# A decoder layer on one core: the last norm's weights in the places of finished activations, and program order on three engines in the down projection's column passes

## The chip, the cores and the metric

The kernel runs on one NeuronCore of a Trainium2 chip. The metric is the device time of one execution in microseconds; the median of three runs before the change is 1082.98. A core has TensorE (PE, the matmuls), VectorE (DVE), ScalarE (ACT), GpSimd (POOL) and SyncE (SP, which here only issues DMAs). They run side by side and wait for each other through semaphores. Each takes its own instructions strictly in the order in which they were put into its queue, so a waiting instruction holds everything behind it on its engine.

## The reference, cut to what matters

```python
# x: (1, 256, 2048) float32; D_FF = 5632
x = x + rmsnorm(mix, post_mix_g)               # after the attention sub-layer
h = rmsnorm(x, pre_ffn_g)
u = causal_dwconv(h @ w_up, conv_w, conv_b)    # width 3 over the tokens
gate, val = jnp.split(u, 2, axis=-1)
y = (jax.nn.gelu(gate, approximate=True) * val) @ w_down    # (256, 5632) @ (5632, 2048)
x = x + rmsnorm(y, post_ffn_g)                 # post_ffn_g: the last norm's weights
```

## The kernel before, in words

Every float32 product is made of three products of split numbers: a weight tile is cast on ACT to a high part (`whi`), DVE subtracts that from the raw tile and gives a low part (`wlo`), and PE adds high x high, high x low and low x high (`product`, L992). So each loaded weight tile costs one DMA issued by SP, one cast on ACT (L333) and one subtraction on DVE (L334) before PE can use it.

The MLP is worked through in two halves of 22 row tiles of `w_down`. In each half, 11 groups of up projection, convolution, GELU and gate give 22 tiles `G` of activations (128 x 512, high and low part of 256 tokens), which take the 22 places of a tag of that name. Then comes the half's column stage: two passes (`column_pass`, L995 on), each over 1024 of the 2048 output columns. A pass goes over 11 pairs of G tiles in an order that is written out. Six pairs (`FAST`) use a scheme of seven products instead of eight block products (`seven`): the pair needs four weight forms, `b11` (512 wide), `f13`, `b2` and `f24` (1024 wide). `prepare` makes them: three loads, one of them of sums of weight rows that were formed in DRAM earlier; `f13` is split from it, then DVE adds to the same tile in place (L1019, L1020), and `f24` is split from the result, so the cast of `f24` waits for DVE and the subtraction for that cast. The other five pairs are plain: two loads, two splits, 24 matmuls. The last pair of a pass (the last three in the very last pass, `HOLD`) is held back and multiplied afterwards one output block at a time (`block`), so that each of the four output banks (`late`) is complete while PE goes on.

Four other banks (`m1`, `m5`, `m7`, `m6`) belong to the fast pairs alone. When the last fast pair, 7, is done, `add_early` adds them into the output `y_sb`: one copy on ACT, then four DVE operations in the first half, eight in the second. In the passes that hold one pair, the next pair's weights are prepared ahead of that; in the very last pass, `add_early` comes at the end of `run`, behind all the preparing. After a pass that is not the last, `ahead` prepares the next pass's first pair; then the four blocks follow, each with a DVE sum into `y_sb` (in the second half with a square on ACT, L1122).

Loads go in turn into five buffers `raw`, one `extra` and two `spare`; split weights go in turn into five pairs `whi`/`wlo` and further places that are free by then: in both halves the convolution's room (`slots`), in the second half also the place of `hT` (`more`), which held the up projection's input.

What sets the order: PE's instructions keep program order everywhere. For ACT, DVE, POOL and SP a scheduler chooses the order at build time, except where the code says otherwise; from the line `x_back = ...` on, all of them keep program order.

The tail: SP loads the residual (`x_back`, L1231) and then the last norm's weights, one tile of 128 x 2048 with the same row on all partitions (`gbf`, L1233), which takes the place of `hT`. POOL multiplies the output blocks by it (`gain`, L1203), takes the power for the norm (L1218), DVE adds the residual (`finish`, L1222), and SP and ACT issue the output DMAs. These steps are interleaved by hand with the last pass's four blocks; the last block is done in two halves of 256 columns.

Of the kernel before, what the change touches and what calls it, by code (L numbers as in the profile page):

```python
# [8 lines left out]
F32 = mybir.dt.float32  # L9
# [8 lines left out]
P = 128  # L18
# [14 lines left out]
def hybrid_layer(ctx: ExitStack, tc: tile.TileContext, x, pre_mix_g, w_in, b_forget, sinks,  # L33
# [834 lines left out]
    with tc.tile_pool(name="ffn", bufs=1) as fp:  # L868
# [47 lines left out]
        def conv(b, ch, dst_tag):  # L916
            u = ubuf[cnt[0] % NU]
# [7 lines left out]
                           scale=cw[:, 2, ch:ch + 1])  # L925
            dve.scalar_tensor_tensor(y, u[:, 1:257], cw[:, 1, ch:ch + 1], y, op0=ALU.mult,  # L926
# [68 lines left out]
        def column_pass(G, sums, weights, some, order, k00, c0, load, parts, hold=1):  # L995
# [14 lines left out]
            def prepare(u):  # L1010
# [33 lines left out]
            def run(add_early):  # L1044
                early, late = ([bank(tag) for _ in range(4)] for tag in ("acc", "att"))
                banks.extend(zip(late, (0, 0, 1, 1), (left, right, left, right)))
                for i, u in enumerate(order):
                    forms = ready.pop(u) if u in ready else prepare(u)
                    if u in some:
                        seven(u, forms, *early, *late[:3])  # L1050
                        if u == fast[-1] and hold == 1:
                            nxt = order[i + 1]
                            ready[nxt] = prepare(nxt)
                            add_early(*early)
# [8 lines left out]
                if hold > 1:  # L1063
                    add_early(*early)
# [8 lines left out]
            return ahead, run, block  # L1073

        ysq = [small.tile([P, 5], F32, tag=f"ysq{t}", bufs=1, name=f"ysq{t}") for t in range(2)]
        for half in range(2):
# [5 lines left out]
            for g in range(FHALF // 2):  # L1082
# [41 lines left out]
            slots = fp.tile([P, ROOM], F32R, tag="room", name="slots")  # L1124
            slots = [slots[:, 32 + i * UNIT:32 + (i + 1) * UNIT] for i in range(2)]
            if half:
                more = main.tile([P, 8, UNIT], F32R, tag="hT", name="more")
                slots += [more[:, i, :] for i in range(8)]
            extra = fp.tile([P, UNIT], F32, tag="extra", name="extra")
            spare = fp.tile([P, 2, UNIT], F32, tag="gates", name="spare")  # L1130
            turn = [None] * 5
            turns = turn + [extra] + turn
            turn = [spare[:, 0, :], spare[:, 1, :], extra] + turn
            units = [0]

            def load(src):
                if not turns:
                    turns.extend(turn)
                raw, c = turns.pop(0), src.shape[-1]
                if raw is None:  # L1140
                    return w_load(src, 1, c)[0]
                sp.dma_start(raw[:, :c].rearrange("p (a c) -> p a c", a=1), src)
                return raw

            def parts(src, n):
                i = units[0] % (5 + len(slots) // 2) - 5
                units[0] += 1
                hi, lo = w_parts(n) if i < 0 else [x[:, :n] for x in slots[i * 2:i * 2 + 2]]
                split(hi, lo, src[:, :n])
                return hi, lo  # L1150

            def y_of(t, n):
                return y_sb[:, t, n * 512:(n + 1) * 512]

            def early_sums(n):
                def add(m1, m5, m7, m6):
                    y11, y12, y21, y22 = (y_of(t, n + c) for t in range(2) for c in range(2))
                    if half == 0:
                        act.copy(y11, m1)
                        dve.tensor_tensor(y12, m6, y11, op=ALU.add)  # L1160
                        dve.tensor_tensor(y21, m7, y12, op=ALU.add)
                        dve.tensor_tensor(y12, m5, y12, op=ALU.subtract)
                        dve.tensor_tensor(y22, m5, y21, op=ALU.subtract)
                        return
                    s = fp.tile([P, 512], F32, tag="cst", name="s")
                    act.copy(s, m1)
                    dve.tensor_tensor(y11, s, y11, op=ALU.add)
                    dve.tensor_tensor(s, m6, s, op=ALU.add)
                    dve.tensor_tensor(y12, y12, s, op=ALU.subtract)
                    dve.tensor_tensor(y12, m5, y12, op=ALU.add)  # L1170
                    dve.tensor_tensor(s, m7, s, op=ALU.add)
                    dve.tensor_tensor(y21, s, y21, op=ALU.add)
                    dve.tensor_tensor(s, m5, s, op=ALU.subtract)
                    dve.tensor_tensor(y22, s, y22, op=ALU.add)
                return add

            weights = {u: pair_sums[half, u] for u in FAST}
            passes = [column_pass(G, sums, weights, FAST, order, half * FHALF, n * 512, load, parts,
                                  hold)
                      for n, order, hold in  # L1180
# [115 lines left out]
```

## Time and the profile before

| | us |
|---|---|
| median of 3 runs (1081.89 to 1084.2) | 1082.98 |
| profiled execution, its own time | 1084.41 |
| its span on the chip | 1082.7 |
| first half's column stage | 579.15 to 697.74 |
| second half's column stage | 940.02 to 1056.96 |
| PE's last matmul ends | 1056.96 |

The profile is one execution, taken by the hardware profiler. Times are from the span's start. Rows of a timeline give start, duration, engine, line and operation, output <- input, the count of instructions merged and, in brackets, the idle time before and what ended it. Busy time of pipelined instructions overlaps, so the step from one start to the next says more than a duration.

### The profile page before, as it was taken

The page shows a single profiled execution, that of the slowest core. Times are in us where ns is not written, and L with a number is a line of the kernel's source. Part 1 is how long each engine was busy: PE and PEld are TensorE (multiplying, and loading weights), DVE is VectorE, ACT ScalarE, POOL GpSimd, SP SyncE. Part 2 cuts the span into 40 slices and gives each one's busy share as a digit, 9 for nine tenths or more (in the row PEclk, how much of TensorE's full clock was granted, in tenths as well). Part 3 has the DMA queues.
Part 4 walks back from the last instruction along what each step waited for, and adds up shares of the span by engine and source line. Part 5 has one row for each costly group of instructions (what it writes and reads, how often), then busy time and mean ns, then how long its engine had stood idle before and what let it go on. Part 6 is the DMA issues. An engine that isn't in the chain of part 4 may idle for free.

```text
span 1082.7 us, 16421 instructions
## 1 busy us (share of the span) xinstructions
PE 1048.4 (97%) x5866; PEld 911.0 (84%) x5866; DVE 848.1 (78%) x1389; ACT 648.3 (60%) x1116; POOL 248.2 (23%) x280
## 2 busy tenths in 40 slices
PE   9999999999999999999999989999999999999990
PEld 7899988888889888888888878888888888878880
DVE  5988868886468788787878888768778887889963
ACT  7776757767467666565655645556555665656720
POOL 3254245440131222222221000013131222100004
PEclk9999999999999999999999989999999999999995
DMA  8748678765994987877876757769696866586733
GB/s 292 236 131 236 182 218 254 191 218 160 327 258 145 324 262 223 232 234 232 233 203 201 249 184 259 239 206 250 212 254 201 232 191 198 163 266 230 233 137 117
DMA packets 170798, 238.56 MB, mean 220 GB/s; under 512 B 7996, under 2 KB 132188, under 8 KB 169692
## 3 DMA queue, kind: packets, MB, share of 16 engines
q1 hardware_dynamic: 163184, 222.25, 63.7%
q0 software_dynamic: 6528, 12.58, 7.8%
q10 hardware_dynamic: 1004, 2.68, 0.6%
q8 instruction: 46, 0.75, 0.3%
q14 instruction: 36, 0.29, 0.1%
HBM read 233.14 MB, written 29.38 MB: 242 GB/s over the span
## 4 chain that ended last, share of the span: by engine, by line
PE 86%; DVE 7%; issue 3%; ACT 2%; DMA 1%; POOL 1%; SPq 0%; DVEq 0%; POOLq 0%; ACTq 0%
PE bank_acc L305 15%; PE bank_att L305 13%; PE bank_acc L330 12%; PE bank_att L992 10%; PE bank_acc L311 8%; PE bank_att L311 7%; PE bank_acc L274 7%; PE bank_acc L992 4%; PE bank_acc L279 4%; DVE wlo L334 2%; PE bank_att L496 1%; PE bank_att L531 1%; DVE wlo L136 1%; PE bank_acc L955 1%; DVE slots L334 1%
## 5 line engine op out<-in xcount | busy, mean ns | idle before, releaser
L136 DVE TENSOR_TENSOR wlo<-raw,whi 128x1024 fp32r<-128x1024 f32 (+3 forms) x271 | 331.4, 1235 | 110.1 <-ACT whi L133 103.4
L133 ACT CAST whi<-raw 128x1024 fp32r<-128x1024 f32 (+3 forms) x270 | 273.0, 1029 | 114.5 <-issue 65.5
L922 POOL TENSOR_TENSOR room<-room,rowf 128x256 f32<-128x256 f32 x88 | 99.2, 1147 | 368.5 <-DVE room L921 367.5
L305 PE MATMUL bank_acc<-hT,whi 128*128 128x512 f32 x736 | 173.3, 390 | 0.0
L305 PEld LDWEIGHTS bank_acc<-hT,whi 128*128 128x128 f32 x736 | 136.4, 188 | 27.4
L305 PE MATMUL bank_att<-hT,whi 128*128 128x512 f32 x640 | 150.6, 390 | 0.0
L305 PEld LDWEIGHTS bank_att<-hT,whi 128*128 128x128 f32 x640 | 118.7, 188 | 23.9
L992 PE MATMUL bank_att<-whi,G 128*128 128x512 f32 x298 | 99.4, 394 | 0.0
L924 ACT ACTIVATE room<-room,cw 128x256 f32<-128x256 f32 x88 | 52.9, 602 | 66.3 <-POOL room L922 66.3
L311 PEld LDWEIGHTS bank_acc<-hT,wlo 128*128 128x128 f32 x736 | 89.3, 188 | 2.0
L311 PE MATMUL bank_acc<-hT,wlo 128*128 128x256 f32 x736 | 89.9, 279 | 0.0
L274 PE MATMUL bank_acc<-hT,whi 128*128 128x512 f32 x352 | 88.0, 395 | 0.0
L330 PE MATMUL bank_acc<-whi,oT 128*128 128x512 f32 (+1 forms) x272 | 81.8, 379 | 0.0
L333 ACT CAST whi<-raw 128x1024 fp32r<-128x1024 f32 (+1 forms) x61 | 56.6, 957 | 39.3 <-PE bank_att L992 17.5
L334 DVE TENSOR_TENSOR wlo<-raw,whi 128x1024 fp32r<-128x1024 f32 (+1 forms) x61 | 66.5, 1117 | 16.1 <-ACT whi L333 16.1
L311 PEld LDWEIGHTS bank_att<-hT,wlo 128*128 128x128 f32 x640 | 77.6, 188 | 1.7
L311 PE MATMUL bank_att<-hT,wlo 128*128 128x256 f32 x640 | 77.9, 279 | 0.0
L926 DVE SCALAR_TENSOR_TENSOR room<-room,cw 128x256 f32<-128x256 f32 x88 | 61.4, 700 | 17.0 <-ACT room L924 16.9
L274 PEld LDWEIGHTS bank_acc<-hT,whi 128*128 128x128 f32 x352 | 63.3, 188 | 11.6
L992 PEld LDWEIGHTS bank_att<-whi,G 128*128 128x128 f32 x298 | 57.0, 191 | 12.1
L992 PE MATMUL bank_att<-wlo,G 128*128 128x512 f32 x149 | 58.7, 394 | 0.0
L330 PEld LDWEIGHTS bank_acc<-whi,oT 128*128 128x128 f32 x272 | 50.2, 188 | 9.4
(269 smaller groups left out, 1722.7 us busy)
## 6 DMA issues: line engine op xcount, KB each, us to landing
raw<-in_w_up_dram SPq DMA_DIRECT2D x176, 512.0 KB, 4.7
raw<-in_w_in_dram SPq DMA_DIRECT2D x51, 512.0 KB, 5.6
raw<-in_w_down_dram SPq DMA_DIRECT2D x45, 512.0 KB, 4.9
raw<-in_w_out_dram SPq DMA_DIRECT2D x32, 512.0 KB, 5.7
t<-in_w_down_dram SPq DMA_DIRECT2D x24, 512.0 KB, 7.3
t<-in_w_down_dram POOLq DMA_DIRECT2D x24, 512.0 KB, 8.7
spare<-in_w_down_dram SPq DMA_DIRECT2D x14, 512.0 KB
raw<-in_w_in_dram SPq DMA_DIRECT2D x16, 384.0 KB, 3.4
```

What stands on the lines that cost most here:

```text
L133: i1 = act.copy(hi[:, cs], raw[:, cs])
L136: i2 = dve.tensor_tensor(lo[:, cs], raw[:, cs], hi[:, cs].bitcast(F32), op=ALU.subtract)
L274: pe.matmul(b, parts[u][0][:, a, m * P:(m + 1) * P], hT[:, kt, :], start=(kt == 0), stop=(kt == KT - 1))
L305: pe.matmul(b, parts[u][0][:, a, m * P:(m + 1) * P], hT[:, kt, :], start=(kt == 0), stop=(kt == KT - 1))
L311: pe.matmul(b[:, 256:512], parts[u][1][:, a, m * P:(m + 1) * P], hT[:, kt, 0:256], start=False, stop=False)
L330: pe.matmul(b, a, r[:, cols], start=(first and i == 0), stop=(last and i == 2))
L333: act.copy(hi, src)
L334: dve.tensor_tensor(lo, src, hi.bitcast(F32), op=ALU.subtract)
L922: pool.tensor_tensor(u[:, 2:258], u[:, 2:258], rowf, op=ALU.mult)
L924: act.activation(y, u[:, 2:258], AF.Identity, bias=cw[:, 3, ch:ch + 1], scale=cw[:, 2, ch:ch + 1])
L926: dve.scalar_tensor_tensor(y, u[:, 1:257], cw[:, 1, ch:ch + 1], y, op0=ALU.mult, op1=ALU.add)
L992: pe.matmul(b[:, to] if to else b, a, r[:, cols], start=(first and i == 0), stop=(last and i == 2))
```

## The change

Three things are changed.

1. The last norm's weights are four tiles of 128 x 512 with the tag of `G`, so they take the places of G tiles 0 to 3 of the second half (pairs 0 and 1), and are loaded by four DMAs.
2. From the last group's convolution to the end of each half's column stage, ACT, DVE and SP keep program order. The code that makes the passes, their buffer turns and the early sums is moved up into functions; the turns themselves are the same. In the new order the first pass's pairs 1 and 3 are prepared ahead of the last group's convolution, which is cut into a beginning (copy, sum, POOL's product, activation) and an end, both beginnings first.
3. When pair 7 is done, in every pass the next two pairs of the order are prepared ahead of the early sums (before: the next one, and in the very last pass all). In the very last pass the early sums thereby come ahead of the preparing of pairs 9 and 10. In each pass's first fast pair, `f24` is split ahead of `b2`, as PE uses them in that order there.

```diff
+            return conv_end(*conv_begin(b, ch, dst_tag))
+        def conv_begin(b, ch, dst_tag):
...
             act.activation(y, u[:, 2:258], AF.Identity, bias=cw[:, 3, ch:ch + 1],
                            scale=cw[:, 2, ch:ch + 1])
+            return u, y, ch
+        def conv_end(u, y, ch):
...
-                b2, f24 = (parts(r, UNIT) for r in (r2, r13))
-                return b11, f13, b2, f24
-            def ahead():
-                ready[order[0]] = prepare(order[0])
+                if u == fast[0]:
+                    f24 = parts(r13, UNIT)
+                    return b11, f13, parts(r2, UNIT), f24
+                b2 = parts(r2, UNIT)
+                return b11, f13, b2, parts(r13, UNIT)
+            def ahead(*us):
+                for u in us:
+                    ready[u] = prepare(u)
...
-                        if u == fast[-1] and hold == 1:
-                            nxt = order[i + 1]
-                            ready[nxt] = prepare(nxt)
+                        if u == fast[-1]:
+                            ahead(*order[i + 1:i + 3])
                             add_early(*early)
...
-                if hold > 1:
-                    add_early(*early)
                 return late
...
+                if g == FHALF // 2 - 1:
+                    inner = tc.manual_schedule(engines={mybir.EngineType.Activation,
+                                                        mybir.EngineType.DVE,
+                                                        mybir.EngineType.SP})
+                    inner.__enter__()
+                    passes = column_passes()
+                    passes[0][0](1, 3)
+                    begun = [conv_begin(bv[m], 44 + c0 // P + m, "yv") for m in range(2)]
                 for m in range(2):
-                    y = conv(bv[m], 44 + c0 // P + m, "yv")
+                    if g == FHALF // 2 - 1:
+                        y = conv_end(*begun[m])
+                    else:
+                        y = conv(bv[m], 44 + c0 // P + m, "yv")
...
                 late = run(early_sums(n))
                 if n == 0:
-                    passes[1][0]()
-                elif half:
+                    passes[1][0](0)
+                elif not half:
+                    inner.__exit__(None, None, None)
+                else:
                     dve.tensor_tensor(y_of(1, 3), late[3], y_of(1, 3), op=ALU.add)
                     break
...
-                               gbf[:, n * 512:(n + 1) * 512][:, cs], op=ALU.mult)
+                               gbf[n][:, cs], op=ALU.mult)
...
+        inner.__exit__(None, None, None)
...
-        gbf = main.tile([P, D], F32, tag="hT", name="gbc_ffn")
-        sp.dma_start(gbf, post_ffn_g[0].partition_broadcast(P))
+        gbf = [fp.tile([P, 512], F32, tag="G", bufs=FHALF, name="gbc_ffn") for n in range(4)]
+        for n in range(4):
+            sp.dma_start(gbf[n], post_ffn_g[0][n * 512:(n + 1) * 512].partition_broadcast(P))
```

More of the change, by code (lines that the diff above doesn't have):

```diff
@@ new lines, in column_passes @@
+        def column_passes():
+            paused[0] = True
+            extra = fp.tile([P, UNIT], F32, tag="extra", name="extra")
+            raw_turns[:] = [None] * 5 + [extra] + [None] * 5
+            split_turns[:] = [None] * 5
+            cycles[:] = [extra], None
+            weights = {u: pair_sums[half, u] for u in FAST}
+            return [column_pass(G, sums, weights, FAST, order, half * FHALF, n * 512, load, parts,
+                                hold)
+                    for n, order, hold in
+                    ((0, (1, 3, 0, 2, 4, 8, 5, 6, 7, 9, 10), 1),
+                     (2, (0, 2, 4, 1, 5, 6, 7, 3, 8, 9, 10), HOLD) if half else
+                     (2, (0, 2, 1, 4, 5, 3, 6, 7, 8, 9, 10), 1))]
@@ L1122, in down @@
                 act.activation(junk[:, cs], ys, AF.Square, accum_out=ysq[t][:, i:i + 1])
[L1124 to L1180, printed above, removed]
-                      ((0, (1, 3, 0, 2, 4, 8, 5, 6, 7, 9, 10), 1),
-                       (2, (0, 2, 4, 1, 5, 6, 7, 3, 8, 9, 10), HOLD) if half else
-                       (2, (0, 2, 1, 4, 5, 3, 6, 7, 8, 9, 10), 1))]
-            paused[0] = True
+            more_places()
```

48 lines of the change are left out of this document (added).

## The prediction

> **What bounds the kernel now.** I read the page first, then the busy time by stretches of the two column stages and of the tail, then the timelines of those three places.
>
> ```profile
> span 1082.7 us, 16421 instructions
> PE 1048.4 (97%) x5866; PEld 911.0 (84%) x5866; DVE 848.1 (78%) x1389; ACT 648.3 (60%) x1116; POOL 248.2 (23%) x280
> 579.15:697.74 118.59, 115.66 (x494) 94.38 (x493) 100.89 (x117) 65.23 (x76) 1.99 (x6) 0.97 0.69 230
> 623.00:635.00 12.00, 9.29 (x28) 6.92 (x27) 9.90 (x13) 3.98 (x5) 0.00 (x0) 0.72 0.75 262
> 940.02:1056.96 116.94, 114.38 (x511) 94.24 (x509) 101.75 (x125) 65.63 (x84) 1.79 (x2) 0.99 0.61 207
> 953.00:961.00 8.00, 5.89 (x18) 4.43 (x18) 7.87 (x9) 4.37 (x6) 0.00 (x0) 0.79 0.80 260
> 1056.96:1082.70 25.74, 0.00 (x0) 0.00 (x0) 9.80 (x15) 1.74 (x6) 11.82 (x11) 0.55 0.34 123
> 680.74 17.00 PE bank_att L992 x75
> ```
>
> In the stretches the columns are length, busy time of PE, weight load, DVE, ACT, POOL, then granted clock, DMA share, GB/s. PE bounds the kernel until 1056.96; after it come 25.74 us in which PE does nothing. From the chain, 75 column matmuls take 17.00 us, 0.2267 each. A column stage has two passes; a pass has six seven-product pairs (21 matmuls) and five plain ones (24), 246 in all, so a stage at full clock without waits is 492 x 0.2267 = 111.5 us. The first half's stage takes 118.59: PE waits 118.59 - 115.66 = 2.9, and 4.2 go to the slow clock (0.72 at 623 to 635). The second takes 116.94: 2.6 of waiting, 2.8 of slow clock (0.79 at 953 to 961). DVE, at 101 to 102 us busy, is close behind PE in both stages. So the change can win in three places: two column stages and the tail.
>
> **The tail.**
>
> ```profile
> 1030.49 0.91 SPq L1231 DMA_DIRECT2D x_back<-x_dram  x2
> x_back<-x_dram SPq DMA_DIRECT2D x2, 1024.0 KB, 9.6
> 1056.99 0.33 SPq L1233 DMA_DIRECT2D gbc_ffn<-in_post_ffn_g_dram  x1
> gbc_ffn<-in_post_ffn_g_dram SPq DMA_DIRECT2D x1, 1024.0 KB, 4.7
> 1061.78 4.92 POOL L1203 TENSOR_TENSOR y_sb<-y_sb,gbc_ffn 128x512 f32<-128x512 f32 x4 [118.82 <-DMA gbc_ffn<-in_post_ffn_g_dram]
> 1073.83 0.41 DVE L1121 TENSOR_TENSOR y_sb<-bank_acc,y_sb 128x256 f32<-128x256 f32 x1
> ```
>
> The weights of the last norm lie in hT's place, which holds split weights that the last blocks read; their load leaves only at 1056.99, when PE is done. POOL then multiplies, and DVE, which in order waits for POOL, comes to the last half block's sum only at 1073.83. In G's places the load waits for pairs 0 and 1 of the last pass alone (its first and fourth), so it leaves right behind x_back. SP keeps its place: 1030.5, plus 9.6 for x_back, plus 4.7, gives weights by about 1045. Four issues instead of one add three of 0.33 on SP, with nothing behind them until the outputs. Before PE's end POOL then does six gains (4.92 / 4 = 1.23 each) and one power, under 8 us in some 12, each behind its block's sum. The last half block's sum starts 0.1 after PE's end instead of at 1073.83, that is 1073.83 - 1056.96 - 0.1 = 16.8 us earlier, and what follows (8.9 us to the end) stays. **Term: -16.8.** Its cover is POOL's 4 us of slack; without it the tail gives back what the gains are late, one for one.
>
> **Program order: what one pair costs DVE.**
>
> ```profile
> 954.44 1.21 DVE L334 TENSOR_TENSOR more<-extra,more 128x1024 fp32r<-128x1024 f32 x1
> 955.58 0.67 DVE L334 TENSOR_TENSOR wlo<-raw,whi 128x512 fp32r<-128x512 f32 x1
> 956.18 2.34 DVE L334 TENSOR_TENSOR wlo<-spare,whi 128x1024 fp32r<-128x1024 f32 x2
> 599.75 0.69 DVE L1019 TENSOR_TENSOR spare<-spare 128x512 f32<-128x512 f32 x1
> 600.47 0.69 DVE L1020 TENSOR_TENSOR spare<-spare 128x512 f32<-128x512 f32 x1
> 601.08 1.22 DVE L334 TENSOR_TENSOR slots<-raw,slots 128x1024 fp32r<-128x1024 f32 x1
> 662.94 2.36 DVE L334 TENSOR_TENSOR wlo<-raw,whi 128x1024 fp32r<-128x1024 f32 x2 [1.19 <-ACT whi L333]
> ```
>
> Start to start, a low part of 1024 takes 1.14, one of 512 0.60, the two sums 0.72 + 0.61. A seven-product pair is 0.60 + 3 x 1.14 + 1.33 = 5.35 on DVE (PE 21 x 0.2267 = 4.76), a plain one 2.28 (PE 5.44). Now DVE often idles 1.19 after the sums, waiting for the cast of what it has just summed (662.94). In program order the low part of r2 lies between, and the wait goes, except in each pass's first fast pair, where f24 now comes first: 1.2 there.
>
> ```profile
> 579.12 0.65 ACT L920 COPY room<-bank_acc 128x256 f32<-128x256 f32 x2 [0.49 <-PE bank_acc L305]
> 580.98 0.60 ACT L924 ACTIVATE room<-room,cw 128x256 f32<-128x256 f32 x1 [0.68 <-POOL room L922]
> 580.47 1.02 DVE L334 TENSOR_TENSOR wlo<-raw,whi 128x512 fp32r<-128x512 f32 x1
> 586.88 0.42 DVE L334 TENSOR_TENSOR G<-room,G 128x256 fp32r<-128x256 f32 x1
> ```
>
> The last group's convolution pays. ACT's second copy (0.3 behind the first now) must in order wait behind the first activation, 580.98 + 0.60; DVE's second sum follows it, and low parts no longer fill the gaps (the one at 580.47 did). I count the convolution done 7.5 us after the first column matmul (now 586.88 + 0.42 - 579.15 = 8.1, with three low parts, 2.9 us, inside).
>
> **First stage.** From 7.5, DVE ends pair 0 at 7.5 + 0.4 (first cast) + 6.55 = 14.45, pair 2 at 19.8, the low part of pair 4's r2 (0.60 + 1.14 + 1.33 + 1.14 = 4.2) at 24.0. PE, after the plain pairs 1 and 3 (10.9) and pairs 0 and 2 (9.5), wants it at 20.4 + nine matmuls and one = 22.7. So PE waits 1.4 to 1.7 in three pieces, and thereafter DVE gains. The early sums here are one copy and four DVE operations, 2.5 us, and with two plain pairs ready PE has 10.9 us meanwhile. Stage: 111.5 + 1.7 = 113.2, against 118.59. **Term: -5.4** (0 if the waits clump and the clock halves again; -7.1 with no wait at all).
>
> **Second stage.** Here the early sums have eight DVE operations and each block sum a square on ACT.
>
> ```profile
> 1039.08 0.68 DVE L1167 TENSOR_TENSOR y_sb<-s,y_sb 128x512 f32<-128x512 f32 x1
> 1044.70 0.68 DVE L1121 TENSOR_TENSOR y_sb<-bank_att,y_sb 128x512 f32<-128x512 f32 x1
> 997.81 0.63 ACT L1122 ACTIVATE junk<-y_sb 128x512 bf16<-128x512 f32 x1 [4.48 <-DVE y_sb L1121]
> 998.57 0.63 ACT L1122 ACTIVATE junk<-y_sb 128x512 bf16<-128x512 f32 x1
> ```
>
> The eight take 1044.70 - 1039.08 = 5.6; a square holds ACT 0.76. In the last pass they lay behind all low parts, where they hid under the blocks; now they lie ahead of pairs 9 and 10. DVE's chain from the first column matmul: 7.9 convolution and first cast, 6.55 pair 0, 26.8 five fast pairs, 6.8 plain pairs 8 to 10, 5.6 early sums, 6.55 next pass's pair 0, 2.4 four block sums, 1.9 until ACT, behind its squares, has cast pair 2's first part, 27.3 five fast pairs with small waits for casts, 6.8 pairs 1, 3, 8, 5.6 early sums, 4.6 pairs 9 and 10: 108.8. PE then has two matmuls and three blocks of 18 left, 12.7: 121.5, with hand-offs 121.9 against 116.94. **Term: +5.0.** It shows as waits in three places: 1.6 as in the first stage, about 5.5 round the start of the second pass (the bank of p4 is free only after the third block sum, which is queued behind pair 0's low parts; done at 60.2 + 1.8 = 62.0, where PE, at 55.8 + 1.6 + twelve matmuls, wants it at 60.1), 3.1 in the first block. Bounds: -5.4 if DVE gets ahead so far that nothing waits, +8 if every hand-off is 0.04 longer (some 100 of them).
>
> **The clock.**
>
> ```profile
> 626.55 1.22 PE L992 MATMUL bank_acc<-slots,sums 128*128 128x512 f32 x2 [1.64 <-DVE slots L334]
> 955.71 0.74 PE L992 MATMUL bank_acc<-more,sums 128*128 128x512 f32 x2 [1.42 <-DVE more L334]
> ```
>
> Each cluster of waits that ended here was followed by the slow clock at a price of 4.2 and 2.8. The new waits of about 2.3 and 1.7 are of this size. After the first DVE sets the pace and a slow PE costs nothing; after the second it costs half of what is left. Between 0 and 4.2 I take **+1.0**. The Trainium skill, "TensorE: Matmul & The Clock Gate", section "What's actually happening", states that the clock halves after an idle window of about 3.4 us; by that rule none of these waits would halve it and the sum would be 1.0 lower. The trace disagrees: 8.00 - 5.89 = 2.1 us of waiting at 953 to 961 were enough.
>
> Loads keep their rotation of buffers and SP its order of loads; the DMA shares 0.69 and 0.61 leave room. Moving the definitions costs nothing.
>
> **Sum**, on the profiled execution's 1084.41: -16.8 - 5.4 + 5.0 + 1.0 = -16.2, 1068.2. The median of three, 1082.98, is 1.4 below that execution; I forecast 1082.98 - 16.2 = **1066.8**.
>
> **The rivals.**
> (a) Nothing is late in the second stage: DVE idles less than I count, both stages come near 113. Then its term is -4 to -5: 1082.98 - 16.8 - 5.4 - 4 = 1056.8, up to 1061. For it: DVE's idle time now is mostly the 1.19 waits that go. Against: the early sums' place, and the convolution.
> (b) The waits cost more: the first stage wins nothing and the clock halves at 4.2: 1082.98 - 16.8 + 5.0 + 4.2 = 1075.4; with half the first stage's win 1072.7. For it: DVE is the close second in both stages, and in order no wait of it can be filled.
> (c) The weights are late all the same (a place of G is held until the blocks): the tail stays, 1083.6, no change that can be told.
> (d) Slower: from the second pass of the second stage PE waits for DVE at every pair, and never gets the full clock back. 246 matmuls there take 0.2267 more each if all are at half clock, 56 us; it decides once more than 16.2 / 0.2267 = 71 of them are slow, and with 90 gives 1087. Against: DVE's chain lets PE run unhindered from pair 1 to pair 3 (111 matmuls, 25 us).
>
> ```profile
> L922 POOL TENSOR_TENSOR room<-room,rowf x88: 631/771/1722, 354.0 to 941.8; 128x256 f32<-128x256 f32 x88
> ```
>
> Against (c): the four pairs before are over some 30 us before PE's end, and slow gains alone don't make it. POOL's product took 0.63 to 1.72 for the same shape, so beside DVE a gain may take 1.1 more, 2.3; six are 14 us against some 12, and the tail would give back 2, which is in the range. The Trainium skill, "SBUF — State Buffer", section "Who interferes with whom", states that a DVE operation with two SBUF inputs blocks GpSimd's reads, which agrees with that spread.
>
> **How the numbers follow.** My forecast 0.65, (a) 0.15, (b) 0.12, (c) 0.03, (d) 0.05. The range reaches from (a)'s upper part to (b)'s lower: 1060 to 1073. Within 0.2% (2.2 us, about what a measurement of this kernel can tell from no change): 0.03; faster 0.92; slower 0.05.
>
> **What would show it.** Right: the weights land before 1050; POOL's gains lie beside PE's last blocks; from PE's end to the span's end about 9 us; first stage about 113, second about 122, with PE waiting for DVE at the start of its second pass and in its first block. Wrong: a tail over 12 us; a second stage under 117 (the early sums' place is harmless) or over 126; a first stage over 117.

## The result and the profile after

The changed kernel takes 1076.61 us, the median of 11 runs (1074.96 to 1080.75), against 1083.42 for 11 runs of the kernel before. The ratio is 0.9939, with an interval of 0.9923 to 0.9955: faster, but by some 7 us where 16 were forecast, and outside the range of 1060 to 1073. The profiled execution took 1075.73 us. (One run of kernel 7 below took 1155.14 us at a mean granted clock of 0.849, and its median and ratio are those of the other five runs.)

The page of the kernel after opens like this.

```profile
span 1074.0 us, 16449 instructions
PE 1048.1 (98%) x5866; PEld 906.8 (84%) x5866; DVE 856.1 (80%) x1389; ACT 647.6 (60%) x1116; POOL 249.1 (23%) x280
```

The stretches of the kernel after follow: first half's column stage, second half's, tail. The columns are length, busy time of PE, weight load, DVE, ACT and POOL, then granted clock, DMA share and GB/s.

```profile
580.08:695.33 115.25, 113.00 (x494) 92.05 (x492) 102.65 (x117) 64.57 (x76) 1.76 (x6) 1.00 0.71 235
937.77:1064.19 126.42, 116.16 (x511) 92.20 (x509) 111.99 (x131) 65.75 (x87) 12.99 (x10) 1.00 0.60 205
1064.19:1074.00 9.81, 0.00 (x0) 0.00 (x0) 4.12 (x9) 0.87 (x4) 2.48 (x4) 0.60 0.41 146
```

A stage runs here from its first column matmul to the next matmul of another kind, or to PE's end. By these bounds the first stage took 118.43 before. Between the two profiled executions lie: 0.9 later into the first stage (580.08 against 579.15), -3.2 in it, nothing in the up projection between the stages (242.44 in both), +9.5 in the second stage (126.42 against 116.94), -15.9 in the tail (9.81 against 25.74). The sum is -8.7, which is the change of the span. The tail is as forecast. The second stage gave back more than half of it.

PE's waits of 0.6 us and more in the kernel after, from its timeline (start, duration, operation, count of merged instructions, and in brackets the idle time before it and what ended it), with the matmuls around the longest. Line numbers have moved: L998 is `product` now, L1025 and L1026 the two sums of a fast pair, L1142 the first of the early sums, L1209 a block's sum, L1233 `gain`; L136 makes a low part of the up projection's weights.

```profile
366.02 1.21 PE L311 MATMUL bank_att<-hT,wlo 128*128 128x256 f32 x8 [0.64 <-DVE wlo L136]
...
594.32 0.50 PE L998 MATMUL bank_acc<-wlo,sums 128*128 128x512 f32 x1 [0.77 <-DVE wlo L334]
...
951.94 0.73 PE L998 MATMUL bank_acc<-more,sums 128*128 128x512 f32 x2 [0.76 <-DVE more L334]
...
1000.87 1.66 PE L998 MATMUL bank_att<-more,G 128*128 128x512 f32 x6 [1.00 <-DVE y_sb L1209]
1004.39 0.50 PE L998 MATMUL bank_acc<-more,G 128*128 128x512 f32 x1 [1.18 <-ACT more L333]
...
1009.19 0.50 PE L998 MATMUL bank_att<-wlo,G 128*128 128x512 f32 x1 [0.93 <-DVE wlo L334]
...
1043.69 0.61 PE L998 MATMUL bank_att<-whi,G 128*128 128x512 f32 x2
1046.43 0.50 PE L998 MATMUL bank_att<-wlo,G 128*128 128x512 f32 x1 [2.13 <-DVE wlo L334]
1046.77 0.39 PE L998 MATMUL bank_att<-whi,G 128*128 128x512 f32 x1
1047.00 0.40 PE L998 MATMUL bank_att<-slots,G 128*128 128x512 f32 x1
...
1050.92 0.74 PE L998 MATMUL bank_att<-more,G 128*128 128x512 f32 x2 [1.26 <-DVE more L334]
```

The second stage's waits stand at the three places that were forecast: behind the convolution (951.94), round the start of the second pass (1000.87 to 1009.19; the first is p4's bank, which waits for a block sum), and in the first block (1046.43, 1050.92). The wait at 366.02 is in the up projection, long before any column pass, and was not forecast.

A wait costs PE more than its bracket says. From 1043.69 to 1047.00 PE starts four matmuls, which at 0.2267 each would take 0.91; 2.40 are lost, where the bracket has 2.13. Over the stage's fourteen waits of 0.15 and more the brackets add up to 10.25, and the steps from start to start to 14.2.

What sets the ends of those waits is DVE. Its timeline in the kernel after, for one fast pair in steady state and for the last low parts, and POOL's first gains:

```profile
959.13 1.22 DVE L334 TENSOR_TENSOR wlo<-spare,whi 128x1024 fp32r<-128x1024 f32 x1
960.38 0.69 DVE L1025 TENSOR_TENSOR spare<-spare 128x512 f32<-128x512 f32 x1
961.11 0.69 DVE L1026 TENSOR_TENSOR spare<-spare 128x512 f32<-128x512 f32 x1
961.72 1.22 DVE L334 TENSOR_TENSOR wlo<-spare,whi 128x1024 fp32r<-128x1024 f32 x1
962.99 1.23 DVE L334 TENSOR_TENSOR slots<-spare,slots 128x1024 fp32r<-128x1024 f32 x1
964.13 1.22 DVE L334 TENSOR_TENSOR more<-extra,more 128x1024 fp32r<-128x1024 f32 x1
...
1039.54 0.68 DVE L1142 TENSOR_TENSOR y_sb<-s,y_sb 128x512 f32<-128x512 f32 x1
...
1045.16 1.22 DVE L334 TENSOR_TENSOR wlo<-spare,whi 128x1024 fp32r<-128x1024 f32 x1
1046.30 1.22 DVE L334 TENSOR_TENSOR slots<-extra,slots 128x1024 fp32r<-128x1024 f32 x1
1047.43 3.44 DVE L334 TENSOR_TENSOR more<-raw,more 128x1024 fp32r<-128x1024 f32 x2
1050.80 0.68 DVE L1220 TENSOR_TENSOR y_sb<-bank_att,y_sb 128x512 f32<-128x512 f32 x1
...
1047.65 4.37 POOL L1233 TENSOR_TENSOR y_sb<-y_sb,gbc_ffn 128x512 f32<-128x512 f32 x2 [105.75 <-DMA gbc_ffn<-in_post_ffn_g_dram]
```

Three things are to be seen. The first sum of a fast pair (L1025) starts 1.25 after the low part ahead of it, not 1.14, and `f24`'s low part starts 1.27 after `b2`'s: 0.11 and 0.13 more than the steps that the prediction used, the first in all twelve fast pairs of a stage, the second in the ten where `f24` follows `b2`. The last two low parts take 3.44 together, where two took 2.34 before, and POOL's first two gains lie exactly beside them. And DVE goes on from its last low part at 1050.80, 113.0 after the stage's first matmul; the prediction had 108.8.

### The profile page after: what moved, and what is told of

Same layout as the page of the kernel before. It is cut to its first block, busy times and chain, and to the rows that moved or that the text cites. A ratio compares the mean times of both kernels' runs of the same rounds, so it can differ in the third digit from the quotient of the medians.

```text
span 1074.0 us, 16449 instructions
## 1 busy us (share of the span) xinstructions
PE 1048.1 (98%) x5866; PEld 906.8 (84%) x5866; DVE 856.1 (80%) x1389; ACT 647.6 (60%) x1116; POOL 249.1 (23%) x280
## 4 chain that ended last, share of the span: by engine, by line
PE 74%; DVE 13%; issue 5%; ACT 4%; DMA 2%; POOL 1%; SPq 0%; DVEq 0%; ACTq 0%; POOLq 0%
PE bank_acc L305 14%; PE bank_att L305 13%; PE bank_acc L330 12%; PE bank_acc L311 7%; PE bank_acc L274 7%; PE bank_att L311 7%; PE bank_acc L279 4%; PE bank_att L998 4%; DVE wlo L334 3%; DVE more L334 2%; DMA raw<-in_w_up_dram 1%; ACT whi L333 1%; DVE wlo L136 1%; PE bank_acc L998 1%; PE bank_att L496 1%
## 5 line engine op out<-in xcount | busy, mean ns | idle before, releaser
L136 DVE TENSOR_TENSOR wlo<-raw,whi 128x1024 fp32r<-128x1024 f32 (+3 forms) x271 | 332.3, 1238 | 114.5 <-ACT whi L133 106.6
L998 PE MATMUL bank_att<-whi,G 128*128 128x512 f32 x298 | 98.1, 389 | 0.0
L998 PEld LDWEIGHTS bank_att<-whi,G 128*128 128x128 f32 x298 | 56.0, 188 | 11.4
L998 PE MATMUL bank_att<-wlo,G 128*128 128x512 f32 x149 | 58.9, 395 | 6.0 <-DVE wlo L334 6.0
```

Source lines behind the costliest of these rows:

```text
L136: i2 = dve.tensor_tensor(lo[:, cs], raw[:, cs], hi[:, cs].bitcast(F32), op=ALU.subtract)
L998: pe.matmul(b[:, to] if to else b, a, r[:, cols], start=(first and i == 0), stop=(last and i == 2))
```

## The experiments

The theory is the prediction's mechanism: the tail gains its 16, and the second stage ends when DVE's chain of low parts and early sums lets it. What had to be told apart was which piece of that chain costs what, and whether it is program order as such, or only the places in which four things stand in that order. All times below are medians; ratios are against the kernel before on the same chip, with their intervals. The stage times come from each run's profiled execution.

| kernel | median | ratio | stage 1 | stage 2 | tail | wait near 366 |
|---|---|---|---|---|---|---|
| before | 1083.42 | | 118.43 | 116.94 | 25.74 | none |
| after | 1076.61 | 0.9939 [0.9923, 0.9955] | 115.25 | 126.42 | 9.81 | 0.6 |
| 1 tail alone | 1068.39 | 0.9834 [0.9818, 0.9850] | 118.30 | 116.95 | 9.90 | none |
| 2 order alone | 1091.95 | 1.0052 [1.0039, 1.0065] | 115.24 | 125.28 | 25.60 | 1.2 |
| 3 order in the first half | 1066.52 | 0.9822 [0.9807, 0.9838] | 115.24 | 115.39 | 9.77 | 2.3 |
| 4 early sums last | 1072.61 | 0.9879 [0.9865, 0.9892] | 115.25 | 121.50 | 11.14 | 1.7 |
| 5 as 3, early load | 1066.63 | 0.9834 [0.9816, 0.9852] | 115.47 | 116.98 | 9.83 | none |
| 6 convolution staged | 1077.77 | 0.9932 [0.9910, 0.9953] | 114.28 | 127.85 | 9.81 | 1.0 |
| 7 `b2` first | 1074.08 | 0.9903 [0.9880, 0.9926] | 113.17 | 124.41 | 10.21 | none |
| 8 four mends | 1066.23 | 0.9831 [0.9812, 0.9850] | 112.25 | 118.33 | 10.86 | none |
| 9 first half, mended | 1063.32 | 0.9808 [0.9794, 0.9823] | 112.26 | 116.39 | 9.82 | none |
| 10 gains later | 1075.50 | 0.9924 [0.9910, 0.9937] | 115.22 | 125.98 | 10.62 | 1.2 |
| 11 as 9, sums last | 1063.69 | 0.9812 [0.9796, 0.9828] | 112.25 | 116.10 | 9.75 | 2.1 |
| 12 early load alone | 1077.64 | 0.9942 [0.9925, 0.9958] | 115.48 | 129.08 | 9.86 | none |

The granted clock was 1.00 in these stages, except for 0.97 in the first stage before and of kernel 1, and in the second stage 0.99 (before, 1, 5 and 12), 0.97 (7 and 10) and 0.96 (6).

**1 and 2: the two halves of the change.** Kernel 1 is the kernel before with only the new place of the last norm's weights:

```diff
-        gbf = main.tile([P, D], F32, tag="hT", name="gbc_ffn")
-        sp.dma_start(gbf, post_ffn_g[0].partition_broadcast(P))
+        gbf = [fp.tile([P, 512], F32, tag="G", bufs=FHALF, name="gbc_ffn") for n in range(4)]
+        for n in range(4):
+            sp.dma_start(gbf[n], post_ffn_g[0][n * 512:(n + 1) * 512].partition_broadcast(P))
```

> The kernel before with the last norm's weights in G's places, nothing else. Theory (three separate terms: tail about -16, first stage about -3, second stage about +9): 1083.4 - 16 = 1067.4, within 1.5, and the second column stage stays at 117 to 118. Rival 1 (the weights' earlier load and POOL's gains beside DVE are what lengthens the second stage): the second stage here grows to 121 or more and the time is 1072 or more. Rival 2 (the tail gives little by itself, the program order brings the rest): 1076 or more.

Kernel 2 is the kernel after with that edit undone.

> The kernel after, with the last norm's weights back in hT's place in one load. Theory: the tail is 25.7 again, first stage -3, second stage +8 to +9: 1083.4 + 5 to 6 = about 1089. Rival 1 (second stage lengthened by the weights and gains): second stage about 120, 1083 to 1085. Rival 2 (program order brings the gain): under 1081.

The second stage and the tail, first of kernel 1, then of kernel 2 (same columns as above):

```profile
939.85:1056.80 116.95, 114.39 (x511) 94.22 (x509) 108.56 (x131) 66.47 (x87) 11.40 (x10) 0.99 0.65 222
1056.80:1066.70 9.90, 0.00 (x1) 0.00 (x0) 4.12 (x9) 0.87 (x4) 2.48 (x4) 0.61 0.41 144
```

```profile
939.32:1064.60 125.28, 116.16 (x511) 92.19 (x509) 105.17 (x125) 64.86 (x84) 1.55 (x2) 1.00 0.57 194
1064.60:1090.20 25.60, 0.00 (x0) 0.00 (x0) 9.80 (x15) 1.74 (x6) 11.82 (x11) 0.56 0.33 123
```

The tail alone wins 16.8 (1085.18 to 1068.39 on that chip) and leaves the second stage as it was. Program order alone loses: 1.0052. Its first stage is 3.2 shorter, its second 8.3 longer. So the change as a whole is a good edit and a bad one together, and the good one alone beats it.

**3: program order in the first half only.** In the second half the scheduler orders ACT, DVE and SP again:

```diff
-                    inner.__enter__()
+                    if half == 0:
+                        inner.__enter__()
...
-        inner.__exit__(None, None, None)
         ctx.enter_context(tc.manual_schedule(
```

> The kernel after, with program order on ACT, DVE and SP kept in the first half's column stage only; in the second the scheduler orders them, from the same source. Theory: the second stage comes back to 116 to 119, the first stays at 115: 1083.4 - 16 - 3 = 1064, at most 1067. Rival (the source order of the early sums lengthens the second stage whoever orders it): second stage 122 or more, 1069 or more.

The second stage is 115.39. The loss is thus bound to program order in the second half. The median is only 2 below kernel 1's, within the intervals: 3.1 are won in the first stage and 1.6 in the second, but PE waits 2.3 near 366 us in this profile (below), the granted clock is 0.50 from 369.16 to 372.57 behind that, and the first stage begins 4.5 later than in kernel 1. The 1.6 are no gain of the edit: PE's idle time in the second stage is 2.58 in both kernels to within 0.02, and what differs is the clock.

**4: the early sums behind all preparing in the very last pass.**

```diff
                             ahead(*order[i + 1:i + 3])
-                            add_early(*early)
+                            if hold == 1:
+                                add_early(*early)
...
+                if hold > 1:
+                    add_early(*early)
                 return late
```

> The kernel after, with the very last pass's early sums back behind the preparing of pairs 9 and 10. Theory (DVE's chain sets PE's end, and eight operations of 0.70 lie in it ahead of the last low parts): PE's end 5.0 to 5.6 earlier, 1071 to 1072. Rival (loads or PE's own pace set the end, DVE is only the last to be seen): no more than 1.5 earlier, 1075 or more.

The stage falls by 4.9, to 121.50: this is what the place of the eight DVE operations (5.6 us) costs, with POOL's gains out of the last low parts' way as well (those end at 1045.7, the gains begin at 1049.18). The median falls by 4.0 only: this execution waits 1.7 near 366 us, and the tail is 1.3 longer. The sum of the last block's first half, which began 0.64 ahead of PE's end in the kernel after, begins 0.59 behind it, since POOL's gains start later against PE's end.

**5: kernel 3 with the first load of weight sums issued early,** ahead of the up projection, where the scheduler had put it before the change:

```diff
+        loaded = [fp.tile([P, UNIT], F32, tag="extra", name="extra")]
+        sp.dma_start(loaded[0].rearrange("p (a c) -> p a c", a=1),
+                     pair_sums[0, 0][:, 0:UNIT].rearrange("p (a c) -> p a c", a=1))
```

> Program order in the first half's column stage only, as in the run of that name, and the load of the first stage's first weight sums back where the scheduler had put it before the change, ahead of the up projection. Theory (that one load's place decides whether PE waits for a low part near 366 us): the wait of 2.3 us is gone, the first column stage starts at 579 to 580 instead of 583.7, and the time is 2 to 4 us less than in that run: 1063 to 1064.5. Rival (the wait is chance in a stretch where the DMA queues are full): the wait appears again between 0.5 and 2.5 us, 1066 to 1068.

The wait near 366 is gone and the first stage starts at 579.18 instead of 583.66. But the medians are equal, 1066.63 and 1066.52, so the 2 to 4 us of the theory aren't seen in them. In the profiles the second stage takes 116.98 against 115.39, although ACT and DVE run it in the same order in both, and PE's three waits in it are the same to 0.01 us (0.70, 1.42 and 0.45 against 0.46). What differs is the granted clock behind the wait of 1.42, here for kernel 5 and then for kernel 3, both 16.95 after the stage's start:

```profile
954.04:957.45 3.41, 3.41 (x9) 2.64 (x8) 2.87 (x4) 0.61 (x1) 0.00 (x0) 0.50 0.93 327
```

```profile
958.29:961.70 3.41, 3.41 (x16) 2.82 (x15) 3.38 (x5) 1.83 (x3) 0.00 (x0) 1.00 0.92 350
```

So 3.41 us at half clock cost 1.6 us here: PE ran 9 matmuls in them instead of 16.

**6: the convolution's beginning step by step for both tiles** (copy, sum and product of both ahead of the activations), so that ACT's second copy doesn't stand behind the first activation:

```diff
-                    begun = [conv_begin(bv[m], 44 + c0 // P + m, "yv") for m in range(2)]
+                    for m in range(2):
+                        act.copy(...); dve.tensor_tensor(...); pool.tensor_tensor(...)
+                    for m in range(2):
+                        act.activation(...)
```

> The kernel after, with the last group's convolution begun step by step for both tiles (both copies, sums and products, then both activations). Theory: DVE ends the convolution 1.5 to 1.9 us earlier in each half; the first stage's waits of 2.2 us shrink by about 1.5, the second stage is 1.9 shorter, since DVE's chain sets its end: in all 3 to 3.5 us less than the kernel after (1077 on the same chip as before at 1083.4). Rival (later waits swallow it): under 1 us.

The first stage wins 1.0 of the expected 1.5, but the second stage lost 1.4 in this execution, and the median shows no gain (0.9932 against 0.9939). The second stage's stretches and its last low parts show why:

```profile
994.54:1013.54 19.00, 15.56 (x56) 10.73 (x55) 15.56 (x20) 10.81 (x18) 0.00 (x0) 0.91 0.45 152
1038.54:1053.54 15.00, 11.23 (x38) 7.57 (x37) 14.01 (x15) 3.29 (x4) 3.69 (x2) 0.81 0.57 224
```

```profile
1047.26 4.52 DVE L334 TENSOR_TENSOR more<-raw,more 128x1024 fp32r<-128x1024 f32 x2
```

The granted clock fell to 0.91 and 0.81 on average behind the two clusters of waits (0.50 for 3.41 and for 6.83 us), and the two low parts beside POOL's gains took 4.52.

**7: `b2` split ahead of `f24` in every fast pair,** as before the change.

```diff
-                if u == fast[0]:
-                    f24 = parts(r13, UNIT)
-                    return b11, f13, parts(r2, UNIT), f24
```

> The kernel after, with b2 split ahead of f24 in the first fast pair of each pass too, PE's order unchanged. Theory: DVE waits 1.2 less for a cast in each pass, f24 is ready as early as now: the second stage 2.0 to 2.4 shorter, the first about 1: 3 us less than the kernel after. Rival (PE waits for f24 longer, since it is a low part later): no change or up to 1 us more.

Both stages are 2.0 to 2.1 shorter, the second although its granted clock was 0.97. The wait of 1.2 that the prediction saw in this edit cost its price, 1.12 and 1.17 us of idle DVE in the two passes of the changed kernel's second stage, and nothing was won for it.

**8: the four mends together** (early load, staged convolution, `b2` first, early sums last), with program order kept in both halves.

> The kernel after, with all four mended: early sums last in the very last pass, convolution step by step, b2 ahead of f24, the early load back. Theory (it is these places, not program order as such, that lengthen the second stage): second stage 126.4 - 4.9 - 1.9 - 2.2 = about 117.5, first about 113, start at 579: 1063 to 1065. Rival (program order leaves DVE's waits unfilled whatever the places): second stage over 120, 1068 or more.

First stage 112.25, second 118.33. The median is 1066.23, not 1063 to 1065: the second stage is 0.8 over the sum, and the tail 1.1 longer, as in kernel 4. So most of the second stage's loss was in the places and not in program order as such: 8.1 of 126.42 - 116.94 = 9.5. What stays above the scheduler's 115.4 to 117.0 are waits round the start of the second pass:

```profile
PE bank_att L1002 <- DVE wlo L334: 1.4, 2, 0.9
PE bank_acc L1002 <- ACT more L333: 1.2, 1, 1.2
PE bank_acc L1002 <- DVE more L334: 1.2, 3, 0.5
```

**9 and 11: the mends with program order in the first half alone,** and the same with the early sums last in the text of the second half.

> Program order in the first half alone, with the early load, the convolution in stages and b2 ahead of f24. If the costs found so far simply add: no wait near 366 us; first stage about 112.3 (as with all four places mended, 112.25), against 115.24 with program order in the first half alone; second stage left to the scheduler, 115.4 to 117.0; the tail of the kernel after. That is 1066.6 less about 3: 1062 to 1064, faster than both kernels and than every version so far. Rival, that a second stage left to the scheduler takes up whatever order it is given: the second stage moves by 2 or more and the median stays at 1066 to 1067.

> The kernel of the first-half test with its mends (early load, convolution in stages, b2 ahead of f24), and in the very last pass the early sums behind all preparing, as before the change, in the order that the scheduler is given. If the scheduler places them by its own reckoning whatever the text says: the second stage is within 1 of that other kernel's. If the text's order counts: it is the scheduler's old stage, 116 to 117. Median 1062 to 1065 in both cases.

Kernel 9 has the lowest median of all, 1063.32 (0.9808), 13 us below the change. Its interval overlaps those of kernels 1, 3, 5, 8 and 11, just so with kernel 1. Its three stretches:

```profile
580.49:692.75 112.26, 112.13 (x494) 92.20 (x492) 102.36 (x117) 64.72 (x76) 1.54 (x6) 1.00 0.74 246
935.19:1051.58 116.39, 113.05 (x511) 93.08 (x509) 107.18 (x131) 66.46 (x87) 12.75 (x10) 1.00 0.65 223
1051.58:1061.40 9.82, 0.00 (x0) 0.00 (x0) 4.12 (x9) 0.87 (x4) 2.48 (x4) 0.66 0.41 146
```

In the first stage PE is busy 112.13 of 112.26 us: it no longer has a wait that a timeline lists. Kernel 11's second stage is 116.10, within 0.3 of kernel 9's. That fits both of its outcomes, since kernel 9's stage is between 116 and 117 too. DVE's timeline decides; the first early sum of the last pass, in kernel 9 and then in kernel 11:

```profile
1029.10 0.69 DVE L1145 TENSOR_TENSOR y_sb<-s,y_sb 128x512 f32<-128x512 f32 x1
```

```profile
1034.52 0.69 DVE L1148 TENSOR_TENSOR y_sb<-s,y_sb 128x512 f32<-128x512 f32 x1
```

In kernel 9 the last four low parts lie among the early sums, in kernel 11 ahead of them all. So the scheduler did go by the text. It made no difference to the stage: in neither kernel does PE wait after 1010 us.

**10: POOL's first two gains queued behind its third,** so that they can't run beside DVE's last low parts.

```diff
-        gain(0, 0)
-        gain(0, 1)
         block(0)
         down(0, 2, late[0])
         gain(0, 2)
+        gain(0, 0)
+        gain(0, 1)
```

> The kernel after, with POOL's first two gains queued behind its third, so that none of them runs beside DVE's last low parts. If POOL's gains slow these: the last two low parts (3.44 us for two) come back to about 2.4, PE's last wait for DVE is about 1.1 shorter (1.3 before), the second stage is 125.3 instead of 126.4, the tail keeps its length, and the median is about 1 us lower (1075.5). Rival, that the two low parts are long for another reason: they stay at 3.4 and the stage at 126.4. If POOL has no room later, the tail grows by up to 2 and the median is 1 higher.

DVE's timeline and two stretches of the profile of kernel 10:

```profile
1048.35 2.35 DVE L334 TENSOR_TENSOR more<-raw,more 128x1024 fp32r<-128x1024 f32 x2
```

```profile
1047.30:1053.30 6.00, 5.78 (x17) 4.15 (x18) 4.70 (x6) 0.38 (x1) 0.00 (x0) 0.72 0.16 59
1053.30:1064.70 11.40, 11.38 (x68) 9.95 (x66) 7.16 (x9) 1.79 (x6) 8.83 (x8) 1.00 0.12 46
```

The low parts are back at 2.35, and PE's wait of 1.26 in front of the last of them is gone: POOL's gains were the cause. Kernel 2, which has no gains at that place, agrees: its second stage is 1.14 shorter than the changed kernel's. Of the 1.1, only 0.4 reached the stage here: behind the wait of 2.13 the granted clock was 0.72 over the first of these stretches. The tail is 0.8 longer, which was expected only for the case that POOL has no room. The ratio, 0.9924, can't be told from the changed kernel's 0.9939.

**12: the early load alone,** on the kernel after.

> The kernel after with one edit: the first load of weight sums of each half is issued ahead of the up projection again, as before the change. If moving that load behind the up projection causes the wait near 366 us: no such wait, the first column matmul at 579.2 (580.1 in the kernel after), the stages unchanged (115.25 and 126.4), median about 1 lower, 1075.7. Rival, that the wait comes and goes with the arrival of the load of w_up whatever is queued ahead of it: a wait of 0.5 to 2 there in this profile too, and the median unchanged.

No wait near 366, and the first matmul at 579.44, as the one theory has it. But the second stage is 129.08, and the median is not lower. The timeline of DVE and POOL in kernel 12, and a stretch behind its last wait:

```profile
1047.02 4.54 DVE L334 TENSOR_TENSOR more<-raw,more 128x1024 fp32r<-128x1024 f32 x2
1046.98 3.50 POOL L1239 TENSOR_TENSOR y_sb<-y_sb,gbc_ffn 128x512 f32<-128x512 f32 x2 [105.48 <-DMA gbc_ffn<-in_post_ffn_g_dram]
```

```profile
1052.35:1055.77 3.42, 3.42 (x9) 2.65 (x9) 1.00 (x3) 0.72 (x2) 1.86 (x2) 0.50 0.02 5
```

The stage began 0.4 earlier, and the weights landed at the very start of the two low parts; these took 4.54 instead of 3.44, and half clock for 3.42 us followed. The 1.1 and some 1.5 for the clock (an estimate: it cost 1.6 in kernel 5) are the 2.7 by which the stage is longer.

**What stays open: the wait near 366 us.** It stands in six of the seven profiles in which the load of weight sums is issued late, and in one of the seven in which it is issued early. That one is kernel 11:

```profile
367.60 1.20 PE L311 MATMUL bank_att<-hT,wlo 128*128 128x256 f32 x8 [2.07 <-DVE wlo L136]
```

So the place of that load alone doesn't decide it; kernel 11 falls to the rival that kernel 12's expectation names. In the kernel after and in kernel 3 the cast of an up-projection weight ahead of it starts later than before the change, at 363.66 and 365.59 for 362.64, since its load lands later. What delays that load was not found. The wait itself is 0.6 to 2.3 us long.

## Why the prediction was wrong

**The tail: right.** -16.8 forecast; -15.9 in the profile and -15.8 in that of kernel 1, which has this edit alone. That the median of kernel 1 falls by exactly 16.8 is luck. POOL's gains begin as the weights land, at 1047.65 (forecast 1045), they lie beside the last blocks, and 9.8 us follow PE's end (forecast about 9).

**The second stage: the step that failed.** The mechanism holds: DVE's chain sets PE's end, and PE waits at the three places named. The brackets of its waits even add up as forecast (1.7, 4.8 and 3.7 for 1.6, 5.5 and 3.1), but that is luck: counted from start to start they are 14.2, 4 more. The size was off, +9.5 for a forecast of +5.0, and the stage of 126.42 is just over the 126 that was to show the step wrong. The failing step is "what one pair costs DVE". Its 5.35 counts 1.14 for every low part, a step that was read where the next operation on DVE had nothing to do with the one ahead of it. In program order a sum follows directly on the low part that reads the same tile, 1.25 behind it, and `f24`'s low part waits 0.13 for its cast: 5.6. Over DVE's chain, from the rows of the kernel after:

| piece of DVE's chain | forecast | measured |
|---|---|---|
| to the start of pair 0 | 7.9 | 8.1 |
| pair 0, both passes | 13.1 | 13.8 |
| five fast pairs and three plain, first pass | 33.6 | 34.9 |
| early sums, both passes | 11.2 | 11.2 |
| block sums and the wait behind them | 4.3 | 4.2 |
| five fast pairs and three plain, second pass | 34.1 | 35.2 |
| pairs 9 and 10 | 4.6 | 5.6 |
| sum | 108.8 | 113.0 |

Hand-offs make about 3 of the 4.2. The prediction had bounded them, but at the edge of its range and not in its sum; and 0.04 each for some 100 on top of +5.0 is +9, not the +8 that it set. The last 1.0 is POOL beside the last two low parts. The prediction had seen that POOL gets slower beside DVE, and had priced it for POOL alone; kernels 2 and 10 show that DVE pays too, on the path.

**The first stage: half right.** -3.2 instead of -5.4. PE's idle time fell from 2.94 to 2.25 only; the other 2.5 are the half clock that no longer follows it (granted 0.97 before, 1.00 after). The prediction priced that clock at 4.2, as all that was above 111.5 and the waits. PE's waits come to 2.3 instead of 1.7, and a stage without any wait takes 112.26 (kernel 9), not the 111.5 worked out from 0.2267 a matmul; the remaining 0.7 is what waits cost beyond their brackets. Kernel 7 and kernel 6 show where the waits come from: 2.1 from `f24` ahead of `b2`, 1.0 from the convolution's order.

**The clock: not in this profile.** +1.0 was set, and both stages have 1.00 granted. Other executions did pay: of the eleven, four with a mean granted clock of 0.991 or 0.992 took 1078.6 to 1079.3, and six with 0.995 to 0.998 took 1075.0 to 1076.6 (the eleventh, at 0.995, took 1080.75). Of the later kernels, 5, 6, 7, 10 and 12 have half clock behind waits of the second stage in their profiles. By the Trainium skill, "TensorE: Matmul & The Clock Gate", section "What's actually happening", it takes an idle window of about 3.4 us. The traces disagree, and show more. Within each of the fourteen profiled executions, the changes of the granted clock lie whole multiples of 3.413 us apart, as if on a grid; in kernel 10 they are at 4.17, 1007.68, 1011.10, 1048.64, 1052.06 and 1069.12. On this grid the wait of 2.13 lies differently in kernel 10 (first two rows) and in the kernel after (last two):

```profile
1045.23:1048.64 3.41, 1.12 (x5) 0.64 (x5) 3.38 (x5) 0.00 (x0) 0.00 (x0) 1.00 0.81 317
1048.64:1052.05 3.41, 3.41 (x9) 2.47 (x10) 2.67 (x3) 0.00 (x0) 0.00 (x0) 0.50 0.08 26
```

```profile
1042.23:1045.64 3.41, 2.07 (x10) 1.38 (x8) 3.31 (x6) 0.81 (x1) 0.00 (x0) 1.00 1.00 410
1045.64:1049.05 3.41, 2.28 (x8) 1.28 (x9) 3.41 (x4) 0.00 (x0) 1.40 (x1) 1.00 0.51 197
```

In kernel 10 the whole wait falls into one window of the grid, PE is idle for 2.29 of its 3.41 us, and the next window is at half clock. In the kernel after, a border at 1045.64 divides the wait into windows with 1.34 and 1.13 of idle time, and the clock stays. Over all fourteen profiles, up to PE's last matmul, the thirteen windows followed by a fall of the clock had 1.48 to 2.29 of idle time. Those that weren't had 1.47 or less, but for two in kernel 12 with 1.48 and 1.64 (ends of matmuls are modelled). So some half of a window seems to be enough, and whether a wait of about 2 us costs anything depends on where it falls.

**Not forecast: the wait near 366 us,** 0.6 in the profile. The prediction counted the loads' order as unchanged. It isn't: the first load of weight sums, which the scheduler had issued ahead of the up projection, moved behind it. Whether that is the cause is open.

**The whole miss.** Between the profiles, -8.7 stands against -16.2. The 7.5 are 4.5 in the second stage, 2.2 in the first, 0.9 in the tail and 0.9 ahead of the first stage, less the 1.0 set for the clock. The rest of the 9.8 between 1066.8 and 1076.61 is that the profiled execution before was 1.4 above its median and the one after 0.9 below.

**The rivals.** (b) has the nearest time, 1072.7 to 1075.4, and its reason is half right: in program order a wait of DVE can't be filled. But neither of its two terms came in the profiled execution: the first stage did win, and the clock held. (a), (c) and (d) are out.

## What to carry to other kernels

Split a change that reorders and relocates into its parts before judging it: here one edit was worth 17 us, and the other cost 6 alone and 7 (by the profiles) to 11 (by the ratios) with it. Durations that are read from a schedule in which other work fills the gaps are too short for a schedule that chains the same operations; add the dependent hand-offs, times their number, on the engine that is close second. And before another engine's work is moved into the shadow of the last stage, look at what shares the memory ports with it there, because the work on the path may be what gets slower. Before a stage of two kernels is compared, look at the granted clock in both: here it made 1.6 us of difference between stages that were otherwise the same.

## What the runs showed of the hardware

- A DVE operation that depends on the one just before it on DVE starts 0.11 to 0.12 later than an independent one: 1.25 instead of 1.14 after a 128x1024 low part, 0.73 instead of 0.61 after a 128x512 sum.
- A wait of PE costs about 0.28 more than the idle time in its bracket: 14.2 instead of 10.25 over fourteen waits.
- POOL's product of 128x512 beside DVE's low parts of 128x1024 makes both slower: two low parts took 2.35 alone (kernels 2 and 10), 3.44 when the product began 0.2 after them, and 4.52 to 4.54 when it began with them or before (kernels 6 and 12). Two products took 2.54 alone, and 4.37 and 3.50 to 3.69 in these cases. Both together end 4.6 to 4.8 after the first began, about as long as one after the other (4.9). The Trainium skill, "SBUF — State Buffer", section "Who interferes with whom", has an exclusive lock between the two engines' ports. That fits this.
- The granted clock changes on a grid of 3.413 us within an execution, and falls to half for one or two windows behind a window with about 1.5 us or more of idle PE. So the same wait of 2.13 us at the same place left it at 1.00 in one execution (kernel after) and was followed by 0.50 for 3.41 us in another (kernel 10).
